# Where the split weights lie: buffers 64 bytes larger in a float32 decoder trunk

## The chip, the cores and the metric

The kernel runs on one core of a Trainium2 chip. The metric is the device time of one execution in microseconds (us); lower is better. Before the change it is 2541.85 us, the median of three runs (2541.64 to 2542.08).

## What is computed

A decoder trunk of two layers on 256 tokens of width 2048, all in float32: a Mamba-2 layer with its gated FFN (with a causal convolution of width 3), then keys and values of that stream, then one layer of causal attention with linear distance penalties, and a second FFN. Each sub-layer is followed by a layer norm of `alpha * x + f(x)`. Cut to the shape of it:

```python
def reference(x, ...):
    h = x
    for layer in range(2):
        if layer < 1:
            mix = mamba2_mixer(h, mamba_w_in[0], ..., mamba_w_out[0])
        else:
            mix = moba_cross_attention(h, attn_w_q[0], attn_w_o[0], k_blk, v_blk, k_mean)
        h = layer_norm(ALPHA * h + mix, ln_mix_g[layer], ln_mix_b[layer])
        ffn = conv_ffn(h, ffn_w_up[layer], ffn_conv_w[layer], ffn_conv_b[layer], ffn_w_down[layer])
        h = layer_norm(ALPHA * h + ffn, ln_ffn_g[layer], ln_ffn_b[layer])
        if layer == 0:
            k_blk, v_blk, k_mean = shared_kv(h, w_kv)
    return h
```

Nearly all the work is in the products with the large weights: `mamba_w_in`, `mamba_w_out`, `ffn_w_up`, `ffn_w_down`, `w_kv`, `attn_w_q` and `attn_w_o`.

## The kernel before

The large products are made with TensorE's reduced float32 type (`F32R`). To keep the accuracy, each operand is cut into a high part (the value cast to that type) and a low part (the value less its high part), and three products are summed: high by high, high by low and low by high. Activations are split where they are made, into `hT`, `yT`, `aT` and `gT`, each with a high and a low half of 256 tokens side by side for each 128 rows. The weights are split on the way.

The program is a row of steps (`steps`, 881 of them). A step is a piece of a weight matrix of 128 x 1024 values, 4096 bytes in each partition. `load` (L171) asks for it on SyncE's queue into one of four buffers `raw`. `split` (L181) makes the high part with a copy on ScalarE (ACT, L200) into a buffer `hi` and the low part with a subtraction on VectorE (DVE, L201) into a buffer `lo`; there are four buffers of each (`LA + 1`), used in turn. Then `products` multiplies:

- In chunks of the modes W the weights are stationary. `some` (L241) goes over the 8 blocks of 128 x 128 in `hi`, each with a moving operand of 512 columns (high and low activations, L256), and over the 8 in `lo`, each with 256 columns (high activations, L259). There are 560 such steps, and in most chunks two neighbouring steps are taken together, so that 16 or 32 matmuls of one kind follow each other.
- In chunks of the mode X the activations are stationary and the weights are the moving operand of 512 columns. `half` (L212) makes for each of two blocks the products with `hi` (L222) and `lo` (L223) and then low activations with `hi` (L227), for two halves of the tokens. There are 320 such steps of 12 matmuls each. In the last chunk of each norm the second half is cut into two pieces of 256 columns.
- One step of mode H holds the 64 columns for the time step of the Mamba layer.

Thirteen steps near the ends of the norms (`spare`) are split into a free part of `hT` in place of the buffers `hi` and `lo`.

The order of all instructions is written out by hand (`manual_schedule`): `at`, `amid`, `within` and `beyond` hang the remaining work (convolutions, scans, norms, attention) behind or inside given steps. `splits` (L204) starts the next split in the middle of a step, at most four steps ahead.

The tiles lie in SBUF in the order of their pools: first the small tiles, `hT` and the two buffers `u` of the pool `base`, then `wts` with `raw`, `hi` and `lo`, then four shared buffers `t4k`, then the pool of the stage (`mamba`, `ffn0`, `att`, `ffn1`). Every tile starts at a multiple of 32 bytes.

Of the kernel before, what the change touches and what calls it, by code (L numbers as in the profile page):

```python
# [19 lines left out]
F32R = mybir.dt.float32r  # L20
# [4 lines left out]
P = 128  # L25
# [14 lines left out]
NC = 512  # L40
# [51 lines left out]
def yoco_kernel(ctx: ExitStack, tc: tile.TileContext, x, lmg, lmb, lfg, lfb, x_t, columns, w, out):  # L92
    nc = tc.nc
    base = ctx.enter_context(tc.tile_pool(name="base", bufs=1))
    wts = ctx.enter_context(tc.tile_pool(name="wts", bufs=LA + 1))
# [75 lines left out]
    def load():  # L171
        i = pos["load"]
        if i >= n_steps:
            return
        pos["load"] += 1
        t = wts.tile([P, 2, NC], F32, tag="raw", name="raw", bufs=RAW)
        for e in (slice(0, 1), slice(1, 2)) if i == 0 else (slice(0, 2),):
            nc.sync.dma_start(t[:, e], w[i][:, e])
        raw_t[i] = t

    def split():  # L181
        i = pos["split"]
        pos["split"] += 1
        t = raw_t.pop(i)
        if i in spare:
            h, l = (bufs["h"][:, k:k + 2].rearrange("p k a t -> p k (a t)") for k in (spare[i], spare[i] + 2))
        else:
            h = wts.tile([P, 2, NC], F32R, tag="hi", name="hi")
            l = wts.tile([P, 2, NC], F32R, tag="lo", name="lo")
        hi_t[i], lo_t[i] = h, l  # L190
        if steps[i][0].mode == "H":
            for a, w in enumerate((h, l)):
                v = t[:, a].rearrange("p (k n) -> p k n", k=8)
                w = w.rearrange("p a (k e n) -> p (a k) e n", e=2, n=NC // 8)
                nc.scalar.copy(w[:, :, 0], v)
                nc.vector.tensor_sub(w[:, :, 1], v, w[:, :, 0].bitcast(F32))
            return load()
        for e in ((0,), (1,)) if i < 2 else ((0, 1),):
            sl = slice(e[0], e[-1] + 1)
            nc.scalar.copy(h[:, sl], t[:, sl])  # L200
            nc.vector.tensor_sub(l[:, sl], t[:, sl], h[:, sl].bitcast(F32))  # L201
        load()

    def splits(i, most=2):  # L204

        for _ in range(1 if steps[i][0] in calm else most):
            j = pos["split"]
            ahead = LA + 1 + sum(i <= k < j for k in spare)
            if j < min(i + ahead, n_steps) and (j in spare or sum(k not in spare for k in hi_t) < LA + 1):
                split()  # L210
# [364 lines left out]
    calm.append(chB[0])  # L575
    put_x(0)
    split()
    put_x(2)
    split()
    for p in range(2, 8):  # L580
        amid(p - 2, put_x, 2 * p)
# [626 lines left out]
```

## Time and profile before

| | before |
|---|---|
| median of three runs | 2541.85 us (2541.64 to 2542.08) |
| the profiled execution | 2542.85 us |
| its span, from the first instruction to the last | 2540.5 us |
| TensorE, matmuls busy | 2526.6 us, 99% of the span |
| TensorE, weights loads busy | 2196.5 us, 86% |
| VectorE (DVE) busy | 1659.8 us, 65% |
| ScalarE (ACT) busy | 1363.4 us, 54% |
| DMA, mean rate | 198 GB/s |
| granted TensorE clock, mean | 0.999 |

The profile is of one execution. In its rows PE is TensorE's matmuls, PEld its weights loads, which overlap them. A group's row gives the line, the engine, the operation, the tile written and the tiles read, the count, then the busy time in us, the mean ns of one, and the idle time of the engine just before, with what ended most of it. A matmul's duration reaches from its start to its modelled end, and the next one starts before that; so the distance from start to start, not the duration, says how fast a row of matmuls runs. A timeline row gives the start and the time in us of a run of like instructions. A row of TensorE's waits gives the us in total, the times and the longest.

### The profile page before, as it was taken

The numbers are of one execution on the slowest core, as the hardware profiler recorded it, in microseconds if no ns is written. First come the engines' busy times: TensorE is split into PE (matmuls) and PEld (weight loads), VectorE is DVE, ScalarE is ACT, GpSimd is POOL, SyncE is SP. The second block draws the span as 40 slices with busy tenths as digits, with TensorE's granted clock in tenths as the row PEclk, the third lists the DMA queues.
The fourth block names the chain that finished last, engine by engine and source line by source line (L and its number), as shares of the span: only waits on it lengthen the run. The fifth ranks groups of instructions, "written<-read, shape, count | busy, mean of one in ns | idle before, by whom it ended". The sixth has DMA issues, their size and how long they took to land.

```text
span 2540.5 us, 36084 instructions
## 1 busy us (share of the span) xinstructions
PE 2526.6 (99%) x13983; PEld 2196.5 (86%) x13983; DVE 1659.8 (65%) x2140; ACT 1363.4 (54%) x1788; POOL 76.0 (3%) x96
## 2 busy tenths in 40 slices
PE   9999999999999999999999999999999999999998
PEld 8888888888888888888888888888888888888887
DVE  7878778755666766666445646645767676765545
ACT  6677787643465555554334445544555555554333
POOL 0000000000200000000000200000200000000001
PEclk9999999999999999999999999999999999999999
DMA  7656655666655555556666655457655555566564
GB/s 257 201 189 198 211 189 187 197 210 220 219 195 190 190 188 189 190 184 201 205 231 205 208 192 168 161 169 236 218 188 192 190 188 191 182 198 202 197 229 159
DMA packets 142123, 502.59 MB, mean 198 GB/s; under 512 B 15856, under 2 KB 16368, under 8 KB 141952
## 3 DMA queue, kind: packets, MB, share of 16 engines
q1 hardware_dynamic: 136832, 482.92, 57.8%
q0 software_dynamic: 4832, 16.85, 2.1%
q8 instruction: 109, 1.79, 0.3%
q14 instruction: 62, 0.51, 0.1%
q10 hardware_dynamic: 288, 0.52, 0.1%
HBM read 491.77 MB, written 8.45 MB: 197 GB/s over the span
## 4 chain that ended last, share of the span: by engine, by line
PE 96%; DVE 2%; DMA 1%; ACT 1%; issue 1%; SPq 0%; DVEq 0%; ACTq 0%
PE acc L256 39%; PE acc L259 21%; PE acc L227 11%; PE acc L223 11%; PE acc L222 11%; DVE lo L201 1%; DMA raw<-in_w 1%; PE acc L794 1%; PE tp L227 0%; PE tp L223 0%; PE tp L222 0%; ACT hi L200 0%; PE tp L803 0%; PE acc L777 0%; PE tp L1073 0%
## 5 line engine op out<-in xcount | busy, mean ns | idle before, releaser
L201 DVE TENSOR_TENSOR lo<-raw,hi 128x1024 fp32r<-128x1024 f32 (+1 forms) x869 | 1061.1, 1226 | 750.3 <-ACT hi L200 616.4
L200 ACT CAST hi<-raw 128x1024 fp32r<-128x1024 f32 (+1 forms) x869 | 909.2, 1048 | 855.7 <-PE acc L227 371.8
L256 PE MATMUL acc<-hT,hi 128*128 128x512 f32 x4480 | 1058.8, 391 | 0.4 <-ACT hi L200 0.3
L256 PEld LDWEIGHTS acc<-hT,hi 128*128 128x128 f32 x4480 | 828.2, 188 | 164.9 <-ACT hi L200 1.0
L259 PEld LDWEIGHTS acc<-hT,lo 128*128 128x128 f32 x4480 | 563.0, 191 | 17.3 <-DVE lo L201 1.4
L259 PE MATMUL acc<-hT,lo 128*128 128x256 f32 x4480 | 571.6, 283 | 0.8 <-DVE lo L201 0.7
L223 PE MATMUL acc<-lo,gT 128*128 128x512 f32 (+1 forms) x678 | 254.5, 378 | 0.0
L222 PE MATMUL acc<-hi,gT 128*128 128x512 f32 (+1 forms) x678 | 254.1, 377 | 0.0
L227 PE MATMUL acc<-hi,gT 128*128 128x512 f32 (+1 forms) x678 | 200.8, 377 | 0.0
L223 PEld LDWEIGHTS acc<-lo,gT 128*128 128x128 f32 x678 | 127.6, 188 | 23.3
L222 PEld LDWEIGHTS acc<-hi,gT 128*128 128x128 f32 x678 | 127.6, 188 | 23.1
L227 PEld LDWEIGHTS acc<-hi,gT 128*128 128x128 f32 x678 | 124.9, 188 | 23.7
L223 PE MATMUL acc<-lo,yT 128*128 128x512 f32 (+1 forms) x270 | 98.6, 369 | 0.0
L222 PE MATMUL acc<-hi,yT 128*128 128x512 f32 (+1 forms) x270 | 98.5, 369 | 0.0
L222 PE MATMUL acc<-hi,hT 128*128 128x512 f32 x192 | 78.7, 410 | 0.0
L227 PE MATMUL acc<-hi,yT 128*128 128x512 f32 (+1 forms) x270 | 77.7, 369 | 0.0
L602 DVE TENSOR_TENSOR u<-u,acc 128x512 f32<-128x512 f32 x108 | 73.5, 681 | 2.9 <-ACT u L601 2.0
L223 PE MATMUL acc<-lo,hT 128*128 128x512 f32 x192 | 75.4, 393 | 0.0
L629 DVE SCALAR_TENSOR_TENSOR g<-u,cols,g 128x254 f32<-128x254 f32 (+1 forms) x176 | 73.3, 478 | 2.9 <-ACT g L624 2.8
L629 DVE SCALAR_TENSOR_TENSOR v<-u,cols,v 128x254 f32<-128x254 f32 (+1 forms) x176 | 73.1, 477 | 0.0
L1023 ACT CAST gT<-v 128x512 fp32r<-128x512 f32 x44 | 27.3, 621 | 84.5 <-DVE v L1022 84.5
L460 POOL TENSOR_TENSOR rs<-rs,mhalf 128x1 f32<-128x1 f32 x8 | 7.4, 931 | 2002.1 <-DVE nb L461 2002.1
(222 smaller groups left out, 1908.2 us busy)
## 6 DMA issues: line engine op xcount, KB each, us to landing
raw<-in_w SPq DMA_DIRECT2D x880, 512.0 KB, 3.5
mA<-acum_d POOLq DMA_DIRECT2D x16, 512.0 KB, 6.8
hres<-r POOLq DMA_DIRECT2D x12, 512.0 KB, 7.0
r<-hres SPq DMA_DIRECT2D x12, 512.0 KB, 4.7
eA<-acum_d POOLq DMA_DIRECT2D x16, 128.0 KB, 8.1
r<-in_x SPq DMA_DIRECT2D x4, 512.0 KB, 5.0
gb<-in_ln_mix_g SPq DMA_DIRECT2D x8, 256.0 KB, 5.1
gb<-in_ln_mix_b SPq DMA_DIRECT2D x8, 256.0 KB, 5.3
```

Source lines behind the costliest of these rows:

```text
L200: nc.scalar.copy(h[:, sl], t[:, sl])
L201: nc.vector.tensor_sub(l[:, sl], t[:, sl], h[:, sl].bitcast(F32))
L222: nc.tensor.matmul(a, th, h[:, kk, sl], start=k == 0, stop=False)
L223: nc.tensor.matmul(a, th, l[:, kk, sl], start=False, stop=False)
L227: nc.tensor.matmul(a, ch.x.lo(k)[:, ts], h[:, kk, sl], start=False, stop=k == ch.nk - 1)
L256: nc.tensor.matmul(banks[j], w[:, kk, js], ch.x.both(k), start=begins, stop=ends, skip_group_check=True)
L259: nc.tensor.matmul(banks[j][:, :S], w[:, kk, js], ch.x.hi(k), start=begins, stop=ends, skip_group_check=True)
L460: nc.gpsimd.tensor_tensor(self.rs[:, h, :], self.rs[:, h, :], mhalf[:, 0, :], op=OP.pow)
L602: nc.vector.tensor_add(dst, dst, p[:, :, :S])
L629: nc.vector.scalar_tensor_tensor(d, u[:, i % 2, :S - k], c1(self.at_w, w[n - 1 - k] + self.ia + i), d, op0=OP.mult, op1=OP.add)
L794: nc.tensor.matmul(ps[64 * q:64 * q + 64, c, j * P:(j + 1) * P], G[g]["xdt"][:, c, h * 64:(h + 1) * 64], G[g]["A", c][:, h, :], start=True ...
L1023: nc.scalar.copy(h, v[:, sl])
```

## The change

`split` asks for buffers of 2 * 512 + 16 values in place of 2 x 512, and uses the first 1024 of them in the shape of before.

```diff
         if i in spare:
             h, l = (bufs["h"][:, k:k + 2].rearrange("p k a t -> p k (a t)") for k in (spare[i], spare[i] + 2))
         else:
-            h = wts.tile([P, 2, NC], F32R, tag="hi", name="hi")
-            l = wts.tile([P, 2, NC], F32R, tag="lo", name="lo")
+
+            h = wts.tile([P, 2 * NC + 16], F32R, tag="hi", name="hi")[:, :2 * NC].rearrange("p (a n) -> p a n", a=2)
+            l = wts.tile([P, 2 * NC + 16], F32R, tag="lo", name="lo")[:, :2 * NC].rearrange("p (a n) -> p a n", a=2)
         hi_t[i], lo_t[i] = h, l
```

The addresses in a partition, as the two built programs have them (bytes, and the remainder of 256):

| tile | before | after |
|---|---|---|
| `hT` | 21632 (128) | 21632 (128) |
| `u`, two buffers | 54944, 56992 (160, 160) | the same |
| `raw`, four buffers | 59520, 63616, 67712, 71808 (all 128) | the same |
| `hi`, four buffers | 75904, 80000, 84096, 88192 (all 128) | 75904, 80064, 84224, 88384 (128, 192, 0, 64) |
| `lo`, four buffers | 92288, 96384, 100480, 104576 (all 128) | 92544, 96704, 100864, 105024 (128, 192, 0, 64) |
| the four `t4k` | from 108672 (all 128) | from 109184 (all 128) |
| `yT`, `gT`, `aT` | 125056 (128) | 125568 (128) |
| `gb` of the attention stage | three buffers, all 64 | 512 bytes further, all 64 |

All that lies behind `lo` moves up by 512 bytes. Each of the four buffers of `hi` and of `lo` serves 217 steps. The two programs have the same instructions, in the same order on each engine, of the same shapes; the line numbers behind the change are one higher after it.

## The prediction

> **What bounds the kernel now.** I read the head of the page first, then the chain that ended last, then the costliest groups.
>
> ```profile
> span 2540.5 us, 36084 instructions
> PE 2526.6 (99%) x13983; PEld 2196.5 (86%) x13983; DVE 1659.8 (65%) x2140; ACT 1363.4 (54%) x1788; POOL 76.0 (3%) x96
> PE 96%; DVE 2%; DMA 1%; ACT 1%; issue 1%; SPq 0%; DVEq 0%; ACTq 0%
> PE acc L256 39%; PE acc L259 21%; PE acc L227 11%; PE acc L223 11%; PE acc L222 11%; DVE lo L201 1%; DMA raw<-in_w 1%; PE acc L794 1%; PE tp L227 0%; PE tp L223 0%; PE tp L222 0%; ACT hi L200 0%; PE tp L803 0%; PE acc L777 0%; PE tp L1073 0%
> ```
>
> The chain is TensorE for 96% of the span. The five lines that multiply with the split weights hold 93% of it, and the two instructions that fill the buffers in question, the copy on ACT (L200) and the subtraction on DVE (L201), hold 1% together. So the change can matter in two ways: it changes the spacing of the matmuls, or it slows the fill so far that TensorE begins to wait. Next I read whether TensorE waits at all, by its own waits and by two long stretches.
>
> ```profile
> PE tp L574 <- POOL ident masks.py:199: 1.4, 1, 1.4
> PE acc L259 <- DVE lo L201: 0.7, 1, 0.7
> PE acc L227 <- DVE hT L403: 0.6, 3, 0.2
> 710.00:1160.00 450.00, 450.00 (x2589) 398.32 (x2588) 308.50 (x406) 253.83 (x319) 0.00 (x0) 1.00 0.58 190
> 1160.00:1400.00 240.00, 240.00 (x1173) 203.40 (x1173) 123.74 (x121) 96.92 (x95) 0.00 (x0) 1.00 0.64 211
> ```
>
> The first three rows are the longest waits of TensorE as an array: 1.4 us at the start, and 0.7 and 0.6 us for DVE. The last two rows are the first FFN's up and down projections (columns: stretch, its length, then busy time and count for PE, weights load, DVE, ACT and POOL, then clock, DMA share and GB/s). TensorE is busy for all of both, at full clock, while DVE has 31% or more of its time free and ACT more than that. There the time is the number of matmuls times their spacing, and the spacing is what has to be read next.
>
> ```profile
> 740.89 7.44 PE L256 MATMUL acc<-hT,hi 128*128 128x512 f32 x32
> 748.17 4.00 PE L259 MATMUL acc<-hT,lo 128*128 128x256 f32 x32
> 752.00 0.86 PE L256 MATMUL acc<-hT,hi 128*128 128x512 f32 x3
> 1199.71 0.39 PE L223 MATMUL acc<-lo,gT 128*128 128x512 f32 x1
> ...
> 1202.89 0.39 PE L223 MATMUL acc<-lo,gT 128*128 128x512 f32 x1
> ```
>
> From start to start, 32 matmuls of 512 columns took 748.17 - 740.89 = 7.28 us, 227.5 ns each; 32 of 256 columns took 752.00 - 748.17 = 3.83 us, 119.7 ns each. Here the weights come out of hi and lo and the moving operand out of hT. Where hi or lo is the moving operand (L222, L223, L227; 14 matmuls from the first to the last of the two lower rows), the spacing is (1202.89 - 1199.71)/14 = 227.1 ns, the same. The difference of the two widths gives (227.5 - 119.7)/256 = 0.421 ns per column, so 256 columns are 107.8 ns and 11.9 ns of each matmul are not streaming. Those 11.9 ns are all that a better layout could take from a matmul.
>
> **The change part by part.** No instruction is added, removed or moved: the order on every engine, the shapes and the waits are those of before. What differs is addresses. Buffers of hi and lo grow from 4096 to 4160 bytes, so the ring of four hi buffers has the remainders 128, 192, 0 and 64 of 256, the ring of lo the same again, and everything behind them moves up by 8 x 64 = 512 bytes, which leaves its remainder alone. raw, which the DMA fills, and hT lie ahead and stay. So no transfer changes its target's remainder, and SP's and POOL's queues carry what they carried. hi and lo of one step still share a remainder, since both rings turn together; what is set apart is a step's buffers from its neighbours', and three of four from hT, gT, yT and raw, which stay at 128.
>
> The first term is the fill: 869 copies and 869 subtractions.
>
> ```profile
> L201 DVE TENSOR_TENSOR lo<-raw,hi 128x1024 fp32r<-128x1024 f32 (+1 forms) x869 | 1061.1, 1226 | 750.3 <-ACT hi L200 616.4
> L200 ACT CAST hi<-raw 128x1024 fp32r<-128x1024 f32 (+1 forms) x869 | 909.2, 1048 | 855.7 <-PE acc L227 371.8
> L602 DVE TENSOR_TENSOR u<-u,acc 128x512 f32<-128x512 f32 x108 | 73.5, 681 | 2.9 <-ACT u L601 2.0
> L403 DVE TENSOR_TENSOR hT<-tp,hT 128x512 fp32r<-128x512 f32 x24 | 16.3, 680 | 1.7 <-ACT hT L402 1.7
> 668.56 0.74 DVE L467 SCALAR_TENSOR_TENSOR r<-r,mv,gb 128x512 f32<-128x512 f32 x1
> 1798.34 0.74 DVE L467 SCALAR_TENSOR_TENSOR r<-r,mv,gb 128x512 f32<-128x512 f32 x1
> ```
>
> The kernel before already has DVE operands at other remainders. u lies at 160 of 256 and hT at 128, and the same operation, SBUF with PSUM to SBUF, took 681 and 680 ns. At 668.56 us gb lies at 128 like r, at 1798.34 us it lies at 64 with r still at 128; both took 0.74 us. So neither sharing a remainder nor leaving it moves a DVE instruction by as much as 1%. I price the 869 subtractions at 0, with a bound of 1% (12 ns) either way. For ACT no two rows differ in the remainder alone, and I give it the same 0 and the same 1% (10 ns). What hides these: DVE idles 750 us and ACT 856 us ahead of just these two lines, while TensorE's spacing holds. Without that cover, in the 1% of the chain that they hold (about 25 us), 1% is 0.25 us. Whichever sign, this term is nothing.
>
> The second term is TensorE's reads. Out of the eight buffers come, by the program, the weights of 4480 matmuls of 512 and 4480 of 256 columns, and the moving operand of 3840 matmuls of 512 (320 steps of 12): 12,800, but for 13 steps of the 881 that are split into a free part of hT. The trace before holds no TensorE operand at another remainder than 128, so here the cost isn't shown and has to be bounded from both sides.
>
> ```profile
> L256 PEld LDWEIGHTS acc<-hT,hi 128*128 128x128 f32 x4480 | 828.2, 188 | 164.9 <-ACT hi L200 1.0
> L259 PEld LDWEIGHTS acc<-hT,lo 128*128 128x128 f32 x4480 | 563.0, 191 | 17.3 <-DVE lo L201 1.4
> 679.42 0.60 PE L398 MATMUL tp<-ident,r 128*128 128x128 f32 x4
> L398 PE MATMUL tp<-ident,r 128*128 128x128 f32 x96 | 14.6, 275 | 0.2
> ```
>
> From above, the best case: all 11.9 ns are a clash of the two reads of TensorE that start at the same remainder, weights and moving operand, and three of four buffers escape it. That is 12,800 x 3/4 x 11.9 ns = 114 us less. From below: a start at 64 or 192 makes each read touch one more piece of 128 bytes, in two of the four buffers. One such piece is 32 columns, 32 x 0.421 = 13.5 ns on the 3840 moving reads, half of which are touched: 26 us. For the weights the nearest row is the run of four transposes: 128 columns with a weights load each, (600 - 275)/3 = 108 ns apart, so 128 weights load in 108 ns at most. Five pieces where there were four make 135 ns, which hides behind 227.5 ns but not behind 119.7: 15 ns on half of the 4480, 34 us. Sum 60 us more.
>
> I take 0 for the second term, by the row it is nearest to: the spacing is the same wherever the operands lie within their buffers and whoever else is at work.
>
> ```profile
> 707.70 7.29 PE acc L256 x32
> ...
> 2251.66 7.28 PE acc L256 x32
> ```
>
> These are the first and the last of the 53 runs of 32 among the longest pieces of the chain, 7.28 or 7.29 us each, while ACT and DVE write the next buffers at the same remainder in some of them and not in others. A clash between engines by remainder would show there as a spread, and there is none. The cover of this zero is TensorE's alone: nothing hides a longer spacing, and 1 ns on 12,800 x 3/4 matmuls is 9.6 us.
>
> [...]
>
> Sum: 0 + 0 us. The profiled execution took 2542.85 us, a span of 2540.5 and 2.35 around it; that stays, and as it stands 1.0 us above the median of the three runs, 2541.85, the forecast for the median is 2541.9 us.
>
> **The rivals.** *The clash inside TensorE goes.* Price as above: 114 us, 2428 us; if it is a clash of one nanosecond, 9.6 us, 2532 us. For it: the 11.9 ns are the same at 512 and at 256 columns, as a toll would be that each weights load of one size takes from the stream, and before every pair of operands starts at one remainder. Against it: the two reads advance at different rates (128 weights in about 108 ns, 256 columns in 107.8), so a common start does not keep them together, and a staggered one would not keep them apart. [...]
>
> *Crossing reads cost TensorE.* This is the slower side: reads that start off a multiple of 128 bytes take one piece more. It decides from the point where the weights load outgrows the 256-column matmul, that is from 11 to 12 ns more on the 108. With the weights of L259 alone it is 34 us, 2576 us; with the moving reads too, 60 us, 2602 us. For it: the five lines have no slack in the chain, and the 256-column spacing is only 12 ns above the row of the transposes. Against it: before, starts at 128 of 256 already cross every larger piece, at no visible toll, so only a piece of just this size does harm.
>
> *The change doesn't separate what it means to.* hi and lo of one step keep one remainder, raw keeps its own. If the toll is between the fill's own operands, nothing changes: 2541.9 us, together with the forecast.
>
> **How the numbers follow.** Forecast with the third rival: 0.55, since every row that can be compared is blind to the remainder. Slower by crossing reads: 0.30, the larger of the two sides, since TensorE has no reserve and no row excludes it; two thirds of it below 2577. Faster: 0.15, half of it small. About 0.2% (5 us) is what can be told from no change here, and the forecast's own range is 2541 to 2543. For 8 in 10 the range goes from 2532 (a nanosecond gained on three quarters of the matmuls) to 2577 (the weights of L259 exposed); left out are about 0.08 below and 0.10 above.
>
> **What would show it.** Right: runs of 32 at 7.28 and 3.83 us and X-mode matmuls at 227 ns, DVE 1226 and ACT 1048 ns, TensorE still 96% of the chain. Wrong on the faster side: runs of 32 that differ from step to step with period four, three short ones and one at 7.28. Wrong on the slower side: the 256-column runs above 3.83 us in two of four steps, and weights loads above 191 ns. Wrong in the first term: L201 or L200 longer by more than 1%, and new waits of TensorE for them.

## The result: 0.59% slower, and the profile after

| | before | after |
|---|---|---|
| median | 2541.74 us (2541.61 to 2542.08, 4 runs) | 2557.28 us (2556.63 to 2558.13, 4 runs) |
| ratio, 95% interval | | 1.0059 (1.0047 to 1.0071) |
| the profiled execution, its span | 2542.85, 2540.5 us | 2557.8, 2555.5 us |

The time is inside the range, 15.4 us above the forecast of 2541.9 and 15.5 above the kernel before: the slower side, which had a chance of 0.30. From the page after (head, chain, groups; all line numbers one higher than before):

```profile
span 2555.5 us, 36084 instructions
PE 2541.8 (99%) x13983; PEld 2184.5 (85%) x13983; DVE 1660.0 (65%) x2140; ACT 1360.7 (53%) x1788; POOL 75.9 (3%) x96
...
PE 97%; DVE 2%; ACT 1%; issue 1%; DMA 0%; SPq 0%; DVEq 0%; ACTq 0%
...
L202 DVE TENSOR_TENSOR lo<-raw,hi 128x1024 fp32r<-128x1024 f32 (+1 forms) x869 | 1061.3, 1226 | 762.9 <-ACT hi L201 626.6
L201 ACT CAST hi<-raw 128x1024 fp32r<-128x1024 f32 (+1 forms) x869 | 905.9, 1044 | 874.0 <-PE acc L228 383.0
L257 PE MATMUL acc<-hT,hi 128*128 128x512 f32 x4480 | 1074.0, 394 | 1.0 <-ACT hi L201 1.0
...
L260 PE MATMUL acc<-hT,lo 128*128 128x256 f32 x4480 | 560.3, 280 | 0.1
```

TensorE's busy time grew by 15.2 us, from 2526.6 to 2541.8; the span grew by 15.0. The fill is where it was: DVE 1226 ns as before, ACT 1044 for 1048. TensorE does not wait more either; these are its longest waits as an array:

```profile
PE tp L575 <- POOL ident masks.py:199: 1.4, 1, 1.4
PE acc L257 <- ACT hi L201: 1.0, 1, 1.0
PE acc L228 <- DVE hT L404: 0.6, 3, 0.2
```

So the spacing of the matmuls changed, and not in one direction. The first FFN in the timeline of TensorE, weights stationary, then a stretch with the weights as moving operand:

```profile
743.20 7.57 PE L257 MATMUL acc<-hT,hi 128*128 128x512 f32 x32
750.61 3.89 PE L260 MATMUL acc<-hT,lo 128*128 128x256 f32 x32
754.34 7.57 PE L257 MATMUL acc<-hT,hi 128*128 128x512 f32 x32
...
1206.00 0.39 PE L223 MATMUL acc<-hi,gT 128*128 128x512 f32 x1
...
1211.50 0.39 PE L223 MATMUL acc<-hi,gT 128*128 128x512 f32 x1
```

A run of 32 of 512 columns takes 750.61 - 743.20 = 7.41 us (7.28 before), one of 256 columns 3.73 us (3.83 before). The 24 matmuls from the first to the last of the lower rows are (1211.50 - 1206.00)/24 = 229.2 ns apart (227.1 before). The wide ones became slower (both kinds) and the narrow ones faster.

A run of 32 holds 8 matmuls from each of four steps, so from each of the four buffers. Mean distance from start to start in ns by blocks of 8, worked out from the starts in the traces over 34 or 35 runs between 750 and 1140 us; a position in the run has the same spacing in all of them within 1 ns, the step in which the trace records starts. The distance is the remainder of the weights less that of the moving operand hT, taken modulo 256 bytes:

| run | first block | second | third | fourth |
|---|---|---|---|---|
| 512 columns, before, distance 0 in all | 230.1 | 226.7 | 226.7 | 226.7 |
| 512 columns, after: distance 0, 192, 128, 64 | 229.9 | 230.0 | 232.9 | 232.7 |
| 256 columns, before, distance 0 in all | 119.1 | 120.0 | 120.0 | 120.0 |
| 256 columns, after: distance 128, 64, 0, 192 | 119.1 | 113.8 | 120.0 | 113.3 |

Over the whole trace, the sums of these distances tell where the 15 us came from. "Weights moving" is L222, L223 and L227 with hi or lo (L223, L224 and L228 after); the rest of TensorE's work was 109.6 us before and 109.5 after.

| us | 512 columns, weights stationary | 256 columns, weights stationary | weights moving |
|---|---|---|---|
| before | 1026.6 | 542.3 | 850.1 |
| after | 1041.8 (+15.2) | 531.1 (-11.2) | 861.2 (+11.1) |

The sum is +15.1 us, the whole of the difference.

### The profile page after: what moved, and what is told of

Its sections match the earlier page's. It is cut to its first block, busy times and chain, and to the rows that moved or that the text cites. A ratio compares the mean times of both kernels' runs of the same rounds, so it can differ in the third digit from the quotient of the medians.

```text
span 2555.5 us, 36084 instructions
## 1 busy us (share of the span) xinstructions
PE 2541.8 (99%) x13983; PEld 2184.5 (85%) x13983; DVE 1660.0 (65%) x2140; ACT 1360.7 (53%) x1788; POOL 75.9 (3%) x96
## 4 chain that ended last, share of the span: by engine, by line
PE 97%; DVE 2%; ACT 1%; issue 1%; DMA 0%; SPq 0%; DVEq 0%; ACTq 0%
PE acc L257 40%; PE acc L260 20%; PE acc L228 11%; PE acc L223 11%; PE acc L224 11%; DVE lo L202 1%; PE acc L795 1%; PE tp L223 0%; PE tp L228 0%; PE tp L224 0%; PE tp L804 0%; PE acc L778 0%; PE tp L1074 0%; DVE r L468 0%; PE tp L1108 0%
## 5 line engine op out<-in xcount | busy, mean ns | idle before, releaser
L202 DVE TENSOR_TENSOR lo<-raw,hi 128x1024 fp32r<-128x1024 f32 (+1 forms) x869 | 1061.3, 1226 | 762.9 <-ACT hi L201 626.6
L201 ACT CAST hi<-raw 128x1024 fp32r<-128x1024 f32 (+1 forms) x869 | 905.9, 1044 | 874.0 <-PE acc L228 383.0
L257 PE MATMUL acc<-hT,hi 128*128 128x512 f32 x4480 | 1074.0, 394 | 1.0 <-ACT hi L201 1.0
L260 PEld LDWEIGHTS acc<-hT,lo 128*128 128x128 f32 x4480 | 552.8, 188 | 17.7 <-issue 1.2
L260 PE MATMUL acc<-hT,lo 128*128 128x256 f32 x4480 | 560.3, 280 | 0.1
L223 PE MATMUL acc<-hi,gT 128*128 128x512 f32 (+1 forms) x678 | 255.8, 380 | 0.0
L224 PE MATMUL acc<-lo,gT 128*128 128x512 f32 (+1 forms) x678 | 255.7, 380 | 0.0
L228 PE MATMUL acc<-hi,gT 128*128 128x512 f32 (+1 forms) x678 | 203.5, 381 | 0.0
L224 PEld LDWEIGHTS acc<-lo,gT 128*128 128x128 f32 x678 | 127.3, 188 | 25.7
L223 PEld LDWEIGHTS acc<-hi,gT 128*128 128x128 f32 x678 | 127.4, 188 | 25.6
L228 PEld LDWEIGHTS acc<-hi,gT 128*128 128x128 f32 x678 | 124.7, 188 | 25.9
L223 PE MATMUL acc<-hi,yT 128*128 128x512 f32 (+1 forms) x270 | 99.0, 371 | 0.0
L224 PE MATMUL acc<-lo,yT 128*128 128x512 f32 (+1 forms) x270 | 98.9, 371 | 0.0
L223 PE MATMUL acc<-hi,hT 128*128 128x512 f32 x192 | 79.2, 412 | 0.0
L228 PE MATMUL acc<-hi,yT 128*128 128x512 f32 (+1 forms) x270 | 78.6, 372 | 0.0
L224 PE MATMUL acc<-lo,hT 128*128 128x512 f32 x192 | 75.9, 395 | 0.0
```

The costliest lines, as they stand in the source:

```text
L223: nc.tensor.matmul(a, th, h[:, kk, sl], start=k == 0, stop=False)
L224: nc.tensor.matmul(a, th, l[:, kk, sl], start=False, stop=False)
L228: nc.tensor.matmul(a, ch.x.lo(k)[:, ts], h[:, kk, sl], start=False, stop=k == ch.nk - 1)
L257: nc.tensor.matmul(banks[j], w[:, kk, js], ch.x.both(k), start=begins, stop=ends, skip_group_check=True)
L260: nc.tensor.matmul(banks[j][:, :S], w[:, kk, js], ch.x.hi(k), start=begins, stop=ends, skip_group_check=True)
```

## The experiments

Three theories stood against each other. *Pair*: the spacing depends on the distance of the starts of TensorE's two operands. *Address*: it depends on the remainder of the buffer that is read, by itself. *Fill*: writes and reads of ACT and DVE at other remainders disturb TensorE. Each run's sums stand in the table at the end of this section.

**Everything 64 bytes further.** A wider small tile ahead moves hT, raw, hi, lo and the stages together.

```diff
-    cols = base.tile([P, -(-N_COL // LINE) * LINE], F32, name="cols")
+    cols = base.tile([P, -(-N_COL // LINE) * LINE + 16], F32, name="cols")
```

> hT, raw, hi, lo and the tiles of all stages lie 64 bytes further (remainder 192), so every distance between two of them is that of before. Pair theory (the spacing of matmuls depends on the distance of the starts of TensorE's two operands): as before, 2541.7 us within 0.1%, runs of 32 matmuls at 7.28 us (512 columns) and 3.83 us (256). Address theory (it depends on the remainder of the buffer that is read): as the buffers at 192 of the changed kernel, 113.3 ns for 256 columns (runs of 3.63 us) and 229 ns or more for 512 columns. Fill theory (writes of ACT and DVE at another remainder disturb TensorE's reads): as before.

Measured: 2542.49 us, ratio 1.0003 (0.9993 to 1.0012), runs of 7.28 and 3.83 us:

```profile
751.99 7.44 PE L256 MATMUL acc<-hT,hi 128*128 128x512 f32 x32
759.27 4.00 PE L259 MATMUL acc<-hT,lo 128*128 128x256 f32 x32
763.10 7.44 PE L256 MATMUL acc<-hT,hi 128*128 128x512 f32 x32
```

Moving everything together by 64 bytes changes nothing, so the address theory falls.

**Both hi and lo 64 bytes further.** A small tile of 64 bytes lies between raw and hi, one of 192 behind lo and ahead of what follows, so that only these two change their remainder.

```diff
+            if i == 0:
+                wts.tile([P, 16], F32, tag="gap", name="gap", bufs=1)
             h = wts.tile([P, 2, NC], F32R, tag="hi", name="hi")
             l = wts.tile([P, 2, NC], F32R, tag="lo", name="lo")
+            if i == 0:
+                wts.tile([P, 48], F32, tag="fill", name="fill", bufs=1)
```

> All buffers of hi and lo at 192, all else at 128 as before. Pair theory: runs of 256 columns 3.63 us (113.3 ns), runs of 512 columns 7.33 to 7.47 us (229 to 233.3 ns), hi or lo as the moving operand 229 to 233 ns; time 2541.7 - 30 + (2.5 to 6.6 ns x 4480 = 11 to 30) + (2.5 to 6.6 ns x 3840 = 10 to 25) = 2532 to 2567 us. Address theory: the same. Fill theory: all buffers of hi and lo share one remainder again, so as before, 7.28 and 3.83 us, 2541.7 us.

Measured: 2542.68 us, ratio 1.0002 (0.9992 to 1.0012). The time alone would have spoken for the fill theory; TensorE's timeline of this kernel says otherwise:

```profile
759.03 3.79 PE L263 MATMUL acc<-hT,lo 128*128 128x256 f32 x32
762.66 7.62 PE L260 MATMUL acc<-hT,hi 128*128 128x512 f32 x32
770.12 3.79 PE L263 MATMUL acc<-hT,lo 128*128 128x256 f32 x32
```

The 256-column run takes 762.66 - 759.03 = 3.63 us (-0.20) and the 512-column run 7.46 us (+0.18). Over the trace that is -26.1 us on the one, +23.1 on the other and +2.8 where the weights move: two large effects of opposite sign that cancel.

**lo alone 64 bytes further.** The 64-byte tile goes between hi and lo, the one of 192 bytes stays behind lo.

```diff
             h = wts.tile([P, 2, NC], F32R, tag="hi", name="hi")
+            if i == 0:
+                wts.tile([P, 16], F32, tag="gap", name="gap", bufs=1)
             l = wts.tile([P, 2, NC], F32R, tag="lo", name="lo")
+            if i == 0:
+                wts.tile([P, 48], F32, tag="fill", name="fill", bufs=1)
```

> The four buffers of lo at 192, hi and all else at 128. Pair and address theory: runs of 512 columns stay at 7.28 us, runs of 256 fall to 3.63 us: -6.7 ns x 4480 = -30 us; L223, with lo as the moving operand, +2.5 to +6.6 ns x 1280 = +3 to +8 us; 2515 to 2520 us. Fill theory: hi and lo are written at different remainders, slower than before, at least half of the 15.5 us of the change.

Measured: 2548.51 us, ratio 1.0026 (1.0016 to 1.0035).

```profile
759.31 3.93 PE L263 MATMUL acc<-hT,lo 128*128 128x256 f32 x32
763.08 7.44 PE L260 MATMUL acc<-hT,hi 128*128 128x512 f32 x32
```

No theory had these spacings; the fill theory alone had the sign, with at least 7.75 us more (half of 15.5) where 6.5 were measured. The 256-column runs stood at 117.8 ns (3.77 us), not at 113.3, although lo and hT lay at exactly the addresses of the run before; and where hi and lo are the moving operands in turn, at distances 0 and 64, the spacing rose to 232 to 234 ns for both, that of hi at distance 0 too, +15.3 us in all. So a distance has more than one spacing.

**A scan.** hi and lo start at an offset that differs from chunk to chunk, in steps of 16 bytes; three buffers raw make room.

```diff
-RAW = 4
+RAW = 3
...
+            o = at_off[ch]
-            h = wts.tile([P, 2, NC], F32R, tag="hi", name="hi")
-            l = wts.tile([P, 2, NC], F32R, tag="lo", name="lo")
+            h = wts.tile([P, 2 * NC + 64], F32R, tag="hi", name="hi")[:, o:o + 2 * NC].rearrange("p (a n) -> p a n", a=2)
+            l = wts.tile([P, 2 * NC + 64], F32R, tag="lo", name="lo")[:, o:o + 2 * NC].rearrange("p (a n) -> p a n", a=2)
```

> Look at the spacing against the distance, not at the time: each weight chunk of the FFN's up projections, and each chunk with the weights as moving operand, has hi and lo at its own multiple of 16 bytes from 0 to 240 behind a start at 128; only three buffers raw, so that the wider buffers fit. Pair and address theory: the spacing is a function of the offset, 226.7 and 120 ns at 0, and as in the changed kernel at 64, 128 and 192; offsets that are no multiple of 64 are open. If a read that crosses a piece of 128 bytes costs (the slower rival of the prediction), the spacing of 512 columns is the same at 0 and 128 and worse at all others. Fill theory: no dependence within a chunk, since its buffers share a remainder.

Measured (its time, 2579.45 us, is that of a kernel with three buffers raw and says nothing here): settled blocks of the first FFN, from the starts in the trace, in ns, one distance in each column:

| distance | 0 | 16 | 32 | 64 | 96 | 128 | 144 | 192 | 240 |
|---|---|---|---|---|---|---|---|---|---|
| 512 columns | 226.6 | 226.6 | 233.3 | 233.3 | 234.5 | 233.3 | 233.3 | 228.9 | 228.3 |
| 256 columns | 120.0 | 118.4 | 118.3 | 117.8, then 113.3 | 117.3 | 118.7 | 120.0 | 117.8 | 117.3 |

The spacing changes with the offset, in steps of 16 bytes too, and none of these distances beats 0 for 512 columns. The crossing rival, which had 0 and 128 alike, does not fit (226.6 and 233.3 ns), nor does the fill theory, which had no effect where a chunk's buffers share one offset. At 64 the first of the two runs of 256 columns stood at 117.8 and the second came down to 113.3: again two spacings at one distance. For 512 columns too the table has one of several: behind other offsets, blocks at 192 also stood at 233.4 ns and blocks at 240 at 226.6. The expectation missed at 192 for 256 columns, 117.8 ns against the 113.3 of the changed kernel.

**The halves of the change.** Only hi, then only lo, has 64 bytes more:

```diff
-            h = wts.tile([P, 2, NC], F32R, tag="hi", name="hi")
+            h = wts.tile([P, 2 * NC + 16], F32R, tag="hi", name="hi")[:, :2 * NC].rearrange("p (a n) -> p a n", a=2)
```

```diff
-            l = wts.tile([P, 2, NC], F32R, tag="lo", name="lo")
+            l = wts.tile([P, 2 * NC + 16], F32R, tag="lo", name="lo")[:, :2 * NC].rearrange("p (a n) -> p a n", a=2)
```

> The half of the change that concerns hi: hi at four remainders, lo at 128. Pair theory, with or without history: 512-column runs as in the changed kernel (blocks at about 227 to 233 ns, +3.8 ns on average, 4480 x 3.8 = +17 us), 256-column runs at 120 ns, L222 and L227 with hi as moving operand +4 to +7 ns x 2560 = +10 to +17 us, 2567 to 2576 us, slower than the whole change. Fill theory: about half of the 15.5 us, 2550 us.

> The half of the change that concerns lo: lo at four remainders, hi at 128. Pair theory: 512-column runs at 226.7 ns, 256-column runs as in the changed kernel (blocks 119, 114, 120, 113.3: -3.2 ns x 4480 = -14 us), products with lo or next to it as moving operand +4 ns x 1280 to 3840 = +5 to +15 us: 2532 to 2543 us, not slower than before. Fill theory: about half of the 15.5 us, 2550 us.

Measured: hi alone 2564.89 us, 1.0089 (1.0072 to 1.0106), 22.7 us over before and more than the whole change; that is 2 us below the range expected, since the products with weights moving took 7.5 us more and not 10 to 17. lo alone 2539.69 us, 0.9991 (0.9981 to 1.0000), not slower. The fill theory's 2550 us misses both. The 256-column run of the second:

```profile
979.15 3.91 PE L259 MATMUL acc<-hT,lo 128*128 128x256 f32 x32
982.89 7.45 PE L256 MATMUL acc<-hT,hi 128*128 128x512 f32 x32
```

3.74 us (3.73 in the whole change), with a block at 113.8 and one at 113.3 ns, although hi stays at 128 and lo does not. So the fill theory's reading of the run with lo alone further (hi and lo written at different remainders make 117.8) falls. The stationary terms are the halves' own: +14.8 us from hi, -10.9 from lo, +15.2 and -11.2 in the whole. Where the weights move the halves do not add: +7.5 and +7.9 apart, +11.1 together; hi and lo alternate there.

**lo placed by step.** Since one distance had shown two spacings, a fourth theory joined the three. *History*: the spacing also depends on how a run is entered. lo gets 192 bytes more, which at this growth lets each buffer start at distance 0, 64, 128 or 192 by choice; it stays at distance 0 where it is the moving operand. The rule in the brackets is what differs between four runs:

```diff
-            l = wts.tile([P, 2, NC], F32R, tag="lo", name="lo")
+            k = pos["lo"] = pos.get("lo", -1) + 1
+            ch, s = steps[i]
+            o = ((64 if ch.mode == "W" and s % (4 if ch.paired else 2) else 0) + 192 * k) % 256 // 4
+            l = wts.tile([P, 2 * NC + 48], F32R, tag="lo", name="lo")[:, o:o + 2 * NC].rearrange("p (a n) -> p a n", a=2)
```

First, distance 0 in the first step of a 256-column run and 64 in the others; and 192 in every step (`192 if ch.mode == "W" else 0`):

> hi stays at 128; lo stays at 128 in the chunks where it is the moving operand and in the first step of each run of 256-column matmuls, and lies at 192 in the other steps of such a run. History theory (the spacing of a run depends on the distance of the two operands and on the spacing the run was entered with; a run that starts at distance 0 comes down to 113.3 ns at distance 64, as the second and fourth blocks of the changed kernel did): first block 119 ns, the three others 113.3, 512 columns 226.7: -6.7 ns x about 3040 = -20 us, 2522 us. Fill theory (lo runs were at 117.8 ns in the run with lo alone at 192 because hi and lo are written at different remainders): the three blocks at 117.8 ns, -2.2 ns x 3040 = -7 us, 2535 us.

> hi at 128 always, lo at 128 where it is the moving operand and at 64 (distance 192) in all steps with 256-column matmuls. Pair theory without history: 113.3 ns as in the block at 64 of the changed kernel, -30 us, 2512 us. History theory: entered from 512-column matmuls at distance 0, so it may lock elsewhere, 113 to 118 ns, as distance 64 did: 2512 to 2533 us. Fill theory: 117.8 ns, 2533 us.

Measured: 2535.13 us, 0.9974 (0.9964 to 0.9983), and 2537.76 us, 0.9982 (0.9972 to 0.9991): both faster, both at 117.8 ns. That is the spacing which the fill theory had for both (2535 and 2533 us); against it stand the run with lo alone at four remainders, above, and the next run. It was a miss of the history theory as I had put it, that any run started at distance 0 comes down: distance 64 behind distance 0 does not. What did come down in the halves were 64 behind 128 and 192 behind 0. So these two, `192` in place of `64` in the rule above, and `((64 if s % (4 if ch.paired else 2) else 128) if ch.mode == "W" else 0)`:

> As the run with lo 64 further in all but the first step of a run, but 192 further (remainder 64). History theory (the spacing a run settles at depends on the distance and on the phase it was entered with): the last block of the run with only lo at four remainders went from distance 0 to 192 and settled at 113.3 ns; so the three later blocks at 113.3 ns, -6.7 ns x about 3040 = -20 us, 2522 us. If the distance alone decides: distance 192 settled at 117.8 ns where all steps of a run had it, so 117.8 ns, 2535 us. Fill theory: as distance 64, 2535 us.

> First step of each run of 256-column matmuls with lo 128 further (remainder 0), the others 64 further (192), lo at 128 where it is the moving operand. History theory: the first two blocks of the run with only lo at four remainders, 121 then 113.3 ns, so three blocks at 113.3 ns, 2522 to 2525 us. If the distance alone decides: 117.8 ns as in the run that starts at distance 0, 2535 us.

Measured: 2524.07 us, 0.9929 (0.9915 to 0.9942), and 2526.77 us, 0.9940 (0.9926 to 0.9953). The timeline of the first:

```profile
755.99 3.84 PE L262 MATMUL acc<-hT,lo 128*128 128x256 f32 x32
759.67 7.44 PE L259 MATMUL acc<-hT,hi 128*128 128x512 f32 x32
766.95 3.84 PE L262 MATMUL acc<-hT,lo 128*128 128x256 f32 x32
```

3.68 us for 256 columns, blocks of 119.2, 113.3, 113.3 and 113.3 ns, and 7.28 us for 512 as before. Distance 192 in all steps gave 117.8 and behind one step at distance 0 gives 113.3. Distance 64 shows the same: its three blocks settled at 117.8 to 118.0 ns behind a step at distance 0 and at 113.8, 113.3 and 113.3 behind one at 128, in the second of these runs. So the spacing depends on the distance and on how a run is entered, and the fill theory, which had 2535 us for the first, falls. The first beats both kernels, by 18.2 us the one before.

**raw alone at four remainders.** The same 64 bytes more, on raw: what ACT and DVE read moves, TensorE's operands keep their remainders.

```diff
-        t = wts.tile([P, 2, NC], F32, tag="raw", name="raw", bufs=RAW)
+        t = wts.tile([P, 2 * NC + 16], F32, tag="raw", name="raw", bufs=RAW)[:, :2 * NC].rearrange("p (a n) -> p a n", a=2)
```

> Only raw lies at four remainders, which the DMA fills and which ACT and DVE read; all operands of TensorE at 128 as before. Pair theory: 7.28 and 3.83 us, 2541.9 us within 0.1%. Fill theory: each copy and subtraction now has its operands at different remainders in three of four steps, as in the changed kernel the subtraction's raw against hi and lo, so part of the 15.5 us appears, and ACT and DVE take other than 1050 and 1228 ns.

Measured: 2542.52 us, 1.0000 (0.9991 to 1.0009), 7.28 and 3.83 us, DVE 1228 ns and ACT 1048 ns for the full-size form (1228 and 1050 before). Setting the fill's operands apart costs nothing. hi and lo also came to lie 256 bytes further from hT here, so a distance of 256 does as 0.

**hT alone 64 bytes further.** raw, hi and lo keep their remainders; what lies behind hT moves by 256 bytes.

```diff
+    cols = base.tile([P, -(-N_COL // LINE) * LINE + 16], F32, name="cols")
...
     bufs = {"h": base.tile([P, KD, 2, S], F32R, name="hT")}
+    base.tile([P, 48], F32, name="fill")
```

> raw, hi, lo and the stages stay at 128; only hT lies 64 bytes further (192), so that the distance from moving operand to weights is 192 wherever hT is moving, and from weights to moving operand 192 the other way round where hT is stationary. Nothing that ACT and DVE write in a split has moved, bar the 13 steps split into hT. Pair theory: runs of 512 columns near 233.3 ns, 7.47 us (+6 ns x 4480 = +25 us), runs of 256 columns at 113.3 or 117.8 ns, 3.63 to 3.77 us (-30 to -9 us); products of gT, yT and aT with hi and lo as before, 226.7 ns; 2536 to 2558 us. Address theory (the buffers' own remainder) and fill theory: 7.28 and 3.83 us, 2541.9 us within 0.1%.

Measured: 2534.06 us, 0.9969 (0.9958 to 0.9980). TensorE's timeline:

```profile
979.44 7.49 PE L256 MATMUL acc<-hT,hi 128*128 128x512 f32 x32
986.76 3.93 PE L259 MATMUL acc<-hT,lo 128*128 128x256 f32 x32
990.53 7.49 PE L256 MATMUL acc<-hT,hi 128*128 128x512 f32 x32
997.86 3.79 PE L259 MATMUL acc<-hT,lo 128*128 128x256 f32 x32
1001.49 7.49 PE L256 MATMUL acc<-hT,hi 128*128 128x512 f32 x32
```

Both spacings moved with the other operand alone, so it is the pair. The time is 2 us below the range expected: the 512-column runs took 7.32 us, 228.9 ns, less than the 233.3 I expected, and what the scan had at distance 192. The 256-column runs take 3.77 us and 3.63 us in turn: 117.8 and 113.3 ns at one distance in one kernel.

All runs but the scan, in us. The sums are of one trace each; the measured difference is that of the medians, against the runs of before that were measured with it:

| run | 512, stationary | 256, stationary | weights moving | sum against before | measured |
|---|---|---|---|---|---|
| before | 1026.6 | 542.3 | 850.1 | | |
| the change | 1041.8 | 531.1 | 861.2 | +15.1 | +15.5 |
| all 64 further | 1027.0 | 541.7 | 850.1 | -0.2 | +0.5 |
| hi and lo 64 further | 1049.7 | 516.2 | 852.9 | -0.2 | +0.7 |
| lo 64 further | 1026.2 | 533.0 | 865.4 | +5.6 | +6.5 |
| hi at four | 1041.4 | 541.8 | 857.6 | +21.8 | +22.7 |
| lo at four | 1026.4 | 531.4 | 858.0 | -3.2 | -2.5 |
| lo by step, 0 then 64 | 1026.8 | 535.1 | 850.0 | -7.1 | -7.0 |
| lo by step, 192 | 1031.0 | 532.9 | 850.0 | -5.1 | -4.4 |
| lo by step, 0 then 192 | 1027.8 | 523.2 | 850.0 | -18.0 | -18.2 |
| lo by step, 128 then 64 | 1027.8 | 525.1 | 849.9 | -16.2 | -15.5 |
| raw at four | 1026.1 | 543.1 | 850.1 | +0.3 | +0.3 |
| hT 64 further | 1031.9 | 525.1 | 852.3 | -9.7 | -8.0 |

## Why the prediction was right or wrong

**The bound, and the place.** Right: TensorE is 97% of the chain after, and all of the difference is in the spacing of its matmuls.

**The first term, the fill, at 0.** Right, and shown: ACT and DVE hold their durations (1044 ns for 1048, 1226 for 1226), raw at four remainders changed nothing (2542.52 us, ratio 1.0000), and hT alone, which but for 13 steps leaves the split as it was, changed the time (2534.06 us). The two rows of 0.74 us that stood for a bound of 1% are given to 0.01 us, that is 1.4%; the run with raw at four remainders gives it closer, 1228 ns for 1228.

**The second term, TensorE's reads, at 0.** This is the step that failed. I took 0 "by the row it is nearest to", the 53 runs of 512 columns that all took 7.28 or 7.29 us. That row compares moments in which ACT and DVE write at the same remainder with moments in which they don't, and about the clash with these engines it was right. It says nothing of TensorE's own two operands, which stood at distance 0 in every run of it. The trace held no row with another distance, as the prediction says itself; there an unchanged row is no evidence for 0. The term was +15.2 - 11.2 + 11.1 = +15.1 us. That the time still fell inside 2532 to 2577 was luck: the upper end is the price of slower 256-column matmuls, and these became faster.

**The slower rival, crossing reads.** Right in the sign, wrong in the mechanism. It put 34 us on the 256-column matmuls of L259, and these became 11.2 us faster; its signs, 256-column runs above 3.83 us and weights loads above 191 ns, did not come (3.73 us and 188 ns). It put 26 us on the moving reads, which took 11.1 more, and nothing on the 512-column matmuls of L256, which it held to be covered and which took 15.2 more. A move of everything by 64 bytes, to remainder 192, left the runs at 7.28 and 3.83 us and the time at a ratio of 1.0003, so what counts is not which pieces a read touches. The piece of 128 bytes behind both prices was my supposition; no run shows one.

**The faster rival, a clash inside TensorE.** The place was right and its one sign was wrong. Setting the operands apart does take time out of a matmul, 120.0 to 113.3 ns, but only out of the narrow ones; it adds as much to the wide ones, 226.7 to 233.3 ns. My argument against it, that two reads at different rates cannot be kept together by a common start, failed: the distance of the starts does change the spacing, which then repeats in a fixed pattern (after the change, 229.2 and 237.5 ns in turn in the third block of the 512-column runs). One argument for it was empty too: that the 11.9 ns are the same at 512 and at 256 columns follows from the way they were worked out, one line through two points. And the 11.9 ns were too small, since each run begins with matmuls that have not settled: the settled blocks, 226.7 and 120.0 ns, give 0.417 ns per column and 13.3 ns beyond the columns. The settled spacing changed by 6.6 ns up and 6.7 ns down with the distance between the starts of the two reads; whether a weights load takes anything from the stream no run shows.

**The forecast of no change, 0.55.** What spoke for it was mostly the silence of the trace. The chance of either side should have been larger where the one operand that bounds the kernel had no row.

**Still open.** Which part of TensorE's reading makes one distance dear at 512 columns and cheap at 256 (at distance 64, 233.3 ns for 226.7 and 113.3 for 120.0), and what chooses between 113.3 and 117.8 ns at one distance. That the entry of a run has to do with it is shown (distance 192: 117.8 ns in all steps, 113.3 behind a step at distance 0); by what rule is not. The pair and its distance are shown as the cause of the 15 us, the mechanism inside TensorE is not.

## What to carry to other kernels

Where TensorE bounds a kernel and hardly waits, as here (96% of the chain, 1.4 us the longest wait), the addresses of its two operands against each other can be a parameter of the time: measure start-to-start distances per buffer, not durations, and treat wide and narrow matmuls and the two roles of a buffer apart, because their signs differ and can cancel in the total (+23, -26 and +3 us gave 0 here). Keep a layout that is good for one role and shift only the buffers of the other: moving lo in the 256-column products alone was worth 0.71%, while 64 bytes more on every buffer of hi and lo cost 0.59%. A resource on the bounding engine that the trace shows in one state only has an unknown price, not a price of 0.

## What the runs showed of the hardware

The spacing of TensorE's matmuls, each with a weights load of 128 columns, in the type F32R, depends in this kernel on the distance of the two operands' starts in the partition: with weights from hi or lo and hT moving, 226.7 ns at distance 0 and from there up to 234.5 ns at the others for 512 columns; 120.0 ns at distance 0 and 113.3 to about 120 elsewhere for 256. The common position did not matter at the one shift tried (64 bytes on all tiles: 7.28 and 3.83 us, unchanged). The spacing takes some matmuls to settle (before the change, the first five of a 512-column run took 228.3 to 235.9 ns and those behind them 226.7 on average) and then repeats in a fixed pattern (after it, 229.2 and 237.5 ns in turn at distance 128); at the same distance a run settled at 113.3 or at 117.8 ns, depending on what came before (distance 192 behind a step at distance 0, and in all steps). DVE and ACT showed nothing of the kind: with raw at four remainders against hi and lo the subtraction took 1228 ns and the copy 1048 ns (1228 and 1050 before).
